# Two gate chunks at a time: a third weight sum made by an adding transfer, and kept quads taken back behind the remainders

## The chip, the cores and the metric

The kernel runs on one core of a Trainium2 chip. The metric is device microseconds from start to end of one execution. The core has four compute engines that run side by side, each with its own queue of instructions that are issued in order: TensorE (PE, matmuls), VectorE (DVE), ScalarE (ACT) and GpSimd (POOL). SyncE (SP) issues most of the transfers. A transfer that adds to what lies in its destination is issued by GpSimd here, a plain load by SyncE; both are carried by the core's 16 DMA engines.

## The reference, cut to what matters

One layer of an encoder for 256 tokens of width 2048: an input projection of the normed input h feeds a retention and a gated delta rule; both are gated, merged and projected; then cross-attention and an MLP. The change touches the gates. Each gate is a matmul of h with 2048 columns of the weights, behind which a silu or a sigmoid scales one branch:

```python
proj = h @ w_in
...
yr = jax.nn.silu(rg.astype(f32)) * yr.reshape(b, s, RET_HEADS * RET_DV)
...
yg = jax.nn.silu(gz.astype(f32)) * yg.reshape(b, s, GDN_HEADS * GDN_DV)

merged = jax.nn.sigmoid(gate_a.astype(f32)) * yr + jax.nn.sigmoid(gate_b.astype(f32)) * yg
return merged.astype(h.dtype) @ w_out
```

All data are f32.

## The kernel before

**Numbers in two parts.** To keep f32 precision, each operand of a matmul is split: ScalarE rounds it to a high part (whi, "the rounding"), VectorE subtracts that to get the low part (wlo, "the remainder"), and TensorE runs three matmuls (high by high, high by low, low by high). A half of a raw weight tile, 128 x 1024, so costs ScalarE one instruction and VectorE one, and there are three buffers for high and three for low halves.

**Tiling.** Tokens are two tiles of 128. The weights of the gates (w_chunks) come in chunks of 512 columns, each in four quarters ("quads") of 512 rows, 1 MB a quarter. The input h lies in SBUF as four quads h1[0] to h1[3], already split.

**Two chunks at once (two_chunks, L949).** In four places two chunks that read the same h, of a silu gate and of a sigmoid gate, are computed together. Quads 2 and 3 of both are multiplied plainly (plain, L1009: 24 matmuls of 512 columns for each). Quads 0 and 1 are multiplied by Strassen's scheme in Winograd's form: with the two token tiles, the two quads and the two chunks as 2 x 2 blocks, seven products (product, L1002: 12 matmuls each) stand in for eight. For that, sums of tokens (s_in) and sums of weights are needed. The weight sums are held in two f32 tiles of two halves each, x (xa, xb) and y (ya, yb). There are four of them, named in the argument moved: "x1" is x = chunk 1 quad 0 plus chunk 0 quad 0; "x2" adds chunk 1 quad 1 to x; "x4" adds chunk 0 quad 1 to x; "y" is y = chunk 1 quad 0 plus chunk 1 quad 1. (The signs lie in the token sums and in what is read from them.)

A sum is made in one of two ways. add_to (L973) has VectorE add the raw tile, which is loaded anyway, to x or y: two instructions on 128 x 1024. add_parts (L968) has GpSimd issue two transfers of 512 KB, one for each half, that read the weights from HBM once more and add them to the tile in SBUF. Before the change x2 and x4 are always adding transfers, x1 is one in the last of the four calls alone, and y is always added by VectorE (L1057).

The order in a call is: plain of chunk 0 quad 2; product with b11; product with x after x1; plain of chunk 0 quad 3; product with b22; product with x after x2; plain of chunk 1 quad 2; product with b21; product with y; product with x after x4; plain of chunk 1 quad 3. TensorE's instructions are chained in this order (triple, L995, issue_after).

**The four calls.** of_retention calls two_chunks for j = 1, 2, 3 (the gates of the retention), of_delta_rule for j = 3 (the last call, which follows the third one at once). The last call alone has `before`, which is take_back (L1124): the merged quads of the first three groups of heads were put away as f32 tiles (kept), and take_back(1) to take_back(3) split them again into high and low parts, one ScalarE (L1127) and one VectorE instruction (L1128) on 128 x 1024 each, in new quad buffers. The output projection (w_out, L1222, matmuls at L218) follows the last call and reads the three quads and a fourth one.

**What sets the order of instructions.** A planner orders the instructions of each engine at build time: among those that its model takes as ready, the one of highest priority goes first, and an engine then runs its queue in that order. Rounding, remainder and loads have the highest priority (`high_priority(offset=100000)`), gates a lower one (50000), and the take-backs none. `tc.issue_after(ins)` queues what is traced in it behind `ins` on the same engine. behind() (L95) does so for the newest rounding, remainder and raw load, kept in `latest`.

Of the kernel before, what the change touches and what calls it, by code (L numbers as in the profile page):

```python
# [31 lines left out]
H_RV, H_RG, H_GZ, H_TA, H_TB = 0, 4, 8, 12, 16  # L32
# [22 lines left out]
def trunk(ctx: ExitStack, tc: tile.TileContext, x_f, mem_f, positions, lead_f, small_f, w_blocks, w_chunks, w_ga,  # L55
# [38 lines left out]
    @contextmanager  # L94
    def behind():  # L95

        with ExitStack() as orders:
            for ins in latest.values():
                orders.enter_context(tc.issue_after(ins))
            yield  # L100

    def step():
        if steps and next(steps[0], steps) is steps:
            steps.pop(0)
# [92 lines left out]
    def cols(w, c):  # L197
        return lambda q: w[c, q]
# [79 lines left out]
    def to_feature(src, quad):  # L278

        for f2 in range(2):  # L280
            ps = bank()
            pv = ps.rearrange("p (f s) -> p f s", f=2)
            for f in range(2):
                for t in range(NT):
                    pe.transpose(pv[:, f, t * P:(t + 1) * P], src(t, f2 * 2 + f), ident)
            if not isinstance(quad, tuple):
                act.activation(quad[:, f2 * 2:f2 * 2 + 2, :], pv, AF.Copy)
                continue
            split([a[:, f2 * 2:f2 * 2 + 2, :] for a in quad], pv)
# [656 lines left out]
        vec.tensor_add(sv[:, 3], a12, sv[:, 1])  # L946
        split([a[:, i, :] for a in s_in], xs[:, 1, :])

    def two_chunks(chunks, evacs, before=None, moved=("x2", "x4")):  # L949

# [3 lines left out]
        x, y = ([mx.tile([P, 1024], F32, name=n, tag=tag, bufs=1) for n, tag in these]  # L956
                for these in ((("xa", "kq"), ("xb", "lw")), (("ya", "qk"), ("yb", "tw"))))
        opened, ends = set(), []

        def lines(n, q, h):  # L960
            return w_chunks[chunks[n], q][:, h * 1024:(h + 1) * 1024]
# [6 lines left out]
        def add_parts(to, n, q):  # L968
            with tc.high_priority(offset=100000):
                for h in range(2):  # L970
                    pool.dma_start(to[h], lines(n, q, h), accum_op=ALU.add)

        def add_to(to, src):  # L973
            with tc.high_priority(offset=100000):
                for h in range(2):
                    with tc.issue_after(latest["lo"]):
                        vec.tensor_add(to[h], to[h], src[h])

        def load(n, q):
            raw = wp.tile([P, 4 * 512], F32, name="raw", tag="raw", bufs=3)  # L980
            with tc.high_priority(offset=100000):
                fetched.append(nc.sync.dma_start(raw, w_chunks[chunks[n], q]).ins)
            return raw[:, 0:1024], raw[:, 1024:2048]

        def parted(srcs):
            halves = []
            with tc.high_priority(offset=100000):
                for src in srcs:
                    hi, lo = (h[:, :1024] for h in half_tiles())
                    latest["hi"] = act.activation(hi, src, AF.Copy).ins  # L990
                    latest["lo"] = vec.tensor_sub(lo, src, hi.bitcast(F32)).ins  # L991
                    halves.append([a.rearrange("p (k n) -> p k n", n=512) for a in (hi, lo)])
            return halves

        def triple(o, lhs, rhs, key):  # L995
            for l, r in ((0, 0), (0, 1), (1, 0)):
                with tc.issue_after(ends[-1]) if ends else ExitStack():
                    ins = pe.matmul(o, lhs[l], rhs[r], start=key not in opened, stop=False, skip_group_check=True).ins  # L998
                opened.add(key)
            return ins  # L1000

        def product(o, lhs, srcs, key):  # L1002
            halves = parted(srcs)
            for i in range(4):
                ins = triple(o, lhs(i), [a[:, i % 2, :] for a in halves[i // 2]], key)
            ends.append(ins)
            step()

        def plain(n, q, by_rows=False):  # L1009
            halves = parted(load(n, q))  # L1010
            for c, (i, t) in enumerate([(i, t) for t in range(NT) for i in range(4)] if by_rows else
                                       [(i, t) for i in range(4) for t in range(NT)]):
                ins = triple(own[n][t], [a[:, i, t * P:(t + 1) * P] for a in h1[q]],
                             [a[:, i % 2, :] for a in halves[i // 2]], (n, t))
                if c % 4 == 3:
                    ends.append(ins)
                    step()
# [4 lines left out]
        def summed(c):  # L1022
            return lambda i: [a[:, i, c * P:(c + 1) * P] for a in s_in]

        def kept_sum(tag, ps):
            o = mx.tile([P, 2, 512], F32, name="u", tag=tag, bufs=1)
            act.activation(o[:, 0], ps, AF.Copy)
            return o

        def finish(n, t, more):  # L1030
            with tc.high_priority(offset=50000):
                evacs[n](t, own[n][t], 0, 512, more)

        def others(q):
            if before:
                before(q)

        plain(0, 2)
        load_parts(x, 1, 0)
# [7 lines left out]
            u = kept_sum("vh", shared)  # L1047
        u1, u3 = u[:, 0], u[:, 1]
        product(p5, summed(0), x, "p5")
        add_parts(x, 1, 1)  # L1050
        plain(0, 3)
        load_parts(y, 1, 0)
        if "y" in moved:
            add_parts(y, 1, 1)
        b22 = load(1, 1)
        product(own[1][0], summed(3), b22, (1, 0))
        if "y" not in moved:  # L1057
            add_to(y, b22)
        product(shared, summed(1), x, "shared")
        add_parts(x, 0, 1)  # L1060
        with tc.high_priority(offset=50000):
            d = kept_sum("vl", shared)
        others(1)
        plain(1, 2)
        b21 = load(0, 1)
        product(own[0][0], part(1, 0), b21, (0, 0))
        finish(0, 0, u1)
        product(shared, summed(2), y, "shared")
        with tc.high_priority(offset=50000):
            act.activation(u3, shared, AF.Copy)  # L1070
            vec.tensor_sub(d[:, 0], p5, d[:, 0])
            vec.tensor_sub(d[:, 1], p5, u3)
        product(own[0][1], part(1, 1), x, (0, 1))
        finish(0, 1, u3)
        others(2)
        others(3)
        plain(1, 3, True)
        kept_back.clear()
# [3 lines left out]
    def gates():  # L1082
        def gate_of(ps, f, scale, more):
            th = mx.tile([P, 512], F32, name="gth", tag="gth", bufs=1)
            if more is not None:
                vec.tensor_add(th, ps, more)
                ps = th
            act.activation(th, ps, f, scale=scale)
            return th

        def silu_gate(y):
            def evac(t, ps, c0, c1, more=None):
                th = gate_of(ps, AF.Silu, 1.0, more)
                vec.scalar_tensor_tensor(y[:, t, :], th, 0.5, y[:, t, :], op0=ALU.mult, op1=ALU.mult)
            return evac

        def sig_gate(y, other=None):
            def evac(t, ps, c0, c1, more=None):
                th = gate_of(ps, AF.Tanh, 0.5, more)
                vec.scalar_tensor_tensor(y[:, t, :], th, 1.0, y[:, t, :], op0=ALU.add, op1=ALU.mult)  # L1100
                if other is not None:
                    vec.tensor_add(y[:, t, :], y[:, t, :], other[:, t, :])
            return evac

        def of_retention(j, yr):
            if j in (1, 2, 3):
                two_chunks((H_RG + j, H_TA + j), (silu_gate(yr), sig_gate(yr)))
                return
            chunk(h1, cols(w_chunks, H_RG + j), silu_gate(yr))
            chunk(h1, cols(w_chunks, H_TA + j), sig_gate(yr))  # L1110

        def of_delta_rule(j, yr, yg, quad, before=None):
            if j in (3,):
                two_chunks((H_GZ + j, H_TB + j), (silu_gate(yg), sig_gate(yg, yr)), before, ("x1", "x2", "x4"))
            else:
                chunk(h1, cols(w_chunks, H_GZ + j), silu_gate(yg))
                chunk(h1, cols(w_chunks, H_TB + j), sig_gate(yg, yr), before=before, cuts=2 if before else 1)
            to_feature(lambda t, f: yg[:, t, f * P:(f + 1) * P], quad)

        return of_retention, of_delta_rule  # L1120
# [11 lines left out]
    for j in range(5):  # L1132
# [14 lines left out]
        if j < 4:  # L1147
            yr = mx.tile([P, NT, 512], F32, name="yr", tag="yr", bufs=1)
            yg = mx.tile([P, NT, 512], F32, name="yg", tag="yg", bufs=1)
# [159 lines left out]
    b11, b12, b22, b21 = (a[:, c:c + 8, :].rearrange("p k s -> p (k s)") for a in (rt, tr) for c in (0, 8))  # L1309
# [341 lines left out]
```

## Time and profile before

| | |
|---|---|
| median of 3 runs | 2036.61 us (2036.29 to 2036.93) |
| the profiled execution | 2035.52 us, of which its span 2033.5 |
| TensorE clock granted | 0.999 |
| transfers by SyncE | 406.93 MB, 57.5% of 16 engines' span |
| adding transfers by GpSimd | 18 of 512 KB, 9.44 MB, 2.6% |
| HBM read | 403.38 MB |

The span is cut into instructions with start and length in microseconds. A row of a timeline has the start, the length, the engine, the line of the kernel, the operation, the tiles (written <- read), and in brackets how long the engine stood idle before it and what ended that. TensorE's matmuls overlap, so their lengths exceed the distance of their starts; a delay is read from the starts. In a table of windows each engine has its busy time, and the last two columns are the share of the DMA engines that was busy and what they moved.

### The profile page before, as it was taken

Reading aid. Unit: us, or ns where it says so; the run is one execution under the profiler, and the core shown is the slowest. Engines: PE = TensorE matmul, PEld = TensorE weight load, DVE = VectorE, ACT = ScalarE, POOL = GpSimd, SP = SyncE. Lnnn points to the kernel's source line nnn. Section 1 sums busy time; section 2 is a strip of 40 time slices with the busy share of each in tenths; the row PEclk is TensorE's granted clock in tenths of the full one; section 3 lists DMA queues with packets and bytes.
Section 4 is the critical chain, followed back from the end, with each engine's and each line's share of the span. In section 5 each row is a group of like instructions: output and inputs, shape, how many; then the busy total and the mean of one; then the engine's idle time right before and its main releaser. Section 6 shows DMA issues by size and latency. Waiting matters only on the chain.

```text
span 2033.5 us, 28629 instructions
## 1 busy us (share of the span) xinstructions
PE 2019.9 (99%) x10742; PEld 1739.4 (86%) x10742; DVE 1622.9 (80%) x2513; ACT 1240.5 (61%) x2029; POOL 58.0 (3%) x68
## 2 busy tenths in 40 slices
PE   9999999999999999999999999999999999999998
PEld 7888888988888888888878899888888888888886
DVE  5887788879877887788887766777887887888788
ACT  6655765675567555755655565566557656656665
POOL 0000000000100000000100000000000000000000
PEclk9999999999999999999999999999999999999999
DMA  8678556455845575556876654568546546554661
GB/s 332 214 269 290 178 185 204 156 186 190 256 170 182 193 242 187 187 181 233 233 237 230 211 187 164 172 217 276 207 140 238 214 154 224 193 204 173 238 232 62
DMA packets 83819, 418.89 MB, mean 206 GB/s; under 512 B 16976, under 2 KB 25056, under 8 KB 39392
## 3 DMA queue, kind: packets, MB, share of 16 engines
q1 hardware_dynamic: 80656, 406.93, 57.5%
q0 software_dynamic: 2592, 9.44, 2.6%
q8 instruction: 84, 1.38, 0.3%
q10 hardware_dynamic: 432, 0.69, 0.1%
q14 instruction: 55, 0.45, 0.1%
HBM read 403.38 MB, written 11.55 MB: 204 GB/s over the span
## 4 chain that ended last, share of the span: by engine, by line
PE 92%; DVE 5%; DMA 2%; issue 1%; ACT 1%; POOLq 0%; DVEq 0%; POOL 0%; ACTq 0%
PE s L218 52%; PE s L1397 7%; PE b L1397 7%; PE s L175 5%; PE s L176 5%; PE s L174 5%; PE s L998 3%; DVE wlo L991 1%; DMA xb<-w_chunks 1%; PE b L998 1%; PE s L407 1%; PE s L408 1%; PE s L409 1%; PE b L705 1%; PE b L835 0%
## 5 line engine op out<-in xcount | busy, mean ns | idle before, releaser
L218 PE MATMUL s<-q,whi 128*128 128x512 f32 x2824 | 971.1, 391 | 0.0
L129 ACT ACTIVATE whi<-raw 128x1024 fp32r<-128x1024 f32 x535 | 567.8, 1062 | 421.7 <-PE s L218 224.4
L130 DVE TENSOR_TENSOR wlo<-raw,whi 128x1024 fp32r<-128x1024 f32 x535 | 652.3, 1222 | 215.8 <-ACT whi L129 209.2
L218 PE MATMUL s<-q,wlo 128*128 128x256 f32 x2824 | 764.9, 281 | 0.0
L218 PEld LDWEIGHTS s<-q,whi 128*128 128x128 f32 x2824 | 521.4, 188 | 100.6
L218 PEld LDWEIGHTS s<-q,wlo 128*128 128x128 f32 x2824 | 528.6, 188 | 13.3 <-DVE wlo L130 0.2
L175 PE MATMUL s<-wlo,q 128*128 128x512 f32 x448 | 176.4, 394 | 0.0
L176 PE MATMUL s<-whi,q 128*128 128x512 f32 x448 | 174.6, 390 | 0.0
L174 PE MATMUL s<-whi,q 128*128 128x512 f32 x448 | 159.0, 390 | 0.0
L227 ACT ACTIVATE bo<-s 128x256 f32<-128x256 f32 x192 | 73.2, 381 | 108.8 <-PE s L218 108.8
L1397 PE MATMUL s<-whi,q 128*128 128x512 f32 x384 | 122.1, 389 | 0.0
L228 DVE TENSOR_TENSOR bo<-bo,s 128x256 f32<-128x256 f32 x192 | 79.9, 416 | 40.3 <-ACT bo L227 39.8
L998 PE MATMUL s<-whi,q 128*128 128x512 f32 x320 | 101.4, 390 | 0.0
L174 PEld LDWEIGHTS s<-whi,q 128*128 128x128 f32 x448 | 84.0, 188 | 17.6
L175 PEld LDWEIGHTS s<-wlo,q 128*128 128x128 f32 x448 | 84.2, 188 | 16.9 <-DVE wlo L130 0.3
L176 PEld LDWEIGHTS s<-whi,q 128*128 128x128 f32 x448 | 84.2, 188 | 16.7
L1420 DVE TENSOR_TENSOR wlo<-rt,whi 128x1024 fp32r<-128x1024 f32 x55 | 67.4, 1226 | 35.9 <-ACT whi L1419 35.4
L218 PE MATMUL s<-q,whx 128*128 128x512 f32 x248 | 86.6, 390 | 0.0
L1397 PEld LDWEIGHTS s<-whi,q 128*128 128x128 f32 x384 | 72.1, 188 | 15.0
L1419 ACT ACTIVATE whi<-rt 128x1024 fp32r<-128x1024 f32 x55 | 58.4, 1061 | 41.6 <-PE s L1397 29.3
L991 DVE TENSOR_TENSOR wlo<-raw,whi 128x1024 fp32r<-128x1024 f32 x56 | 67.9, 1222 | 11.8 <-ACT whi L990 11.6
L990 ACT ACTIVATE whi<-raw 128x1024 fp32r<-128x1024 f32 x56 | 59.0, 1059 | 28.6 <-PE s L998 15.7
(403 smaller groups left out, 2975.4 us busy)
## 6 DMA issues: line engine op xcount, KB each, us to landing
raw<-w_ff SPq DMA_DIRECT2D x96, 1024.0 KB
raw<-w_chunks SPq DMA_DIRECT2D x76, 1024.0 KB
raw<-w_blocks SPq DMA_DIRECT2D x64, 1024.0 KB
raw<-w_xk SPq DMA_DIRECT2D x16, 1024.0 KB
raw<-w_out SPq DMA_DIRECT2D x16, 1024.0 KB
raw<-w_xq SPq DMA_DIRECT2D x16, 1024.0 KB
raw<-w_xo SPq DMA_DIRECT2D x16, 1024.0 KB
rt<-w_ff SPq DMA_DIRECT2D x16, 1024.0 KB
```

The costliest lines, as they stand in the source:

```text
L129: latest["hi"] = act.activation(hi[:, cs], src[:, cs], AF.Copy).ins
L130: latest["lo"] = vec.tensor_sub(lo[:, cs], src[:, cs], hi[:, cs].bitcast(F32)).ins
L174: pe.matmul(o, xh, wh, start=first, stop=False)
L175: pe.matmul(o, xh, wl, start=False, stop=False)
L176: pe.matmul(o, xl, wh, start=False, stop=last)
L218: ins = pe.matmul(ps[b][:, :S] if part else ps[b], halves[h][part][:, i, b * P:(b + 1) * P], x[:, kk % 4, :], start=kk == 0 and not part, ...
L227: act.activation(o, ps[b][:, S:], AF.Copy)
L228: vec.tensor_add(o, o, ps[b][:, :S])
L991: latest["lo"] = vec.tensor_sub(lo, src, hi.bitcast(F32)).ins
L998: ins = pe.matmul(o, lhs[l], rhs[r], start=key not in opened, stop=False, skip_group_check=True).ins
L1397: ins = pe.matmul(o, lhs[l], rhs[r], start=key not in opened, stop=last and j == 2, skip_group_check=True).ins
L1420: latest["lo"] = vec.tensor_sub(lo, raw[:, c:c + 1024], hi.bitcast(F32)).ins
```

## The change

The third sum, y, becomes an adding transfer in all four calls: y is in the default of moved, and in the set of the last call, which so has all four. The call of take_back(1) moves from ahead of the plain product of chunk 1 quad 2 to behind the product with y, and all three take-backs are traced inside behind(). The branches on "x2" are new too; every call's set holds "x2".

```diff
-    def two_chunks(chunks, evacs, before=None, moved=("x2", "x4")):
+    def two_chunks(chunks, evacs, before=None, moved=("x2", "x4", "y")):
...
             if before:
-                before(q)
+                with behind():
+                    before(q)
...
         product(p5, summed(0), x, "p5")
-        add_parts(x, 1, 1)
+        if "x2" in moved:
+            add_parts(x, 1, 1)
         plain(0, 3)
         load_parts(y, 1, 0)
         if "y" in moved:
             add_parts(y, 1, 1)
         b22 = load(1, 1)
         product(own[1][0], summed(3), b22, (1, 0))
+        if "x2" not in moved:
+            add_to(x, b22)
         if "y" not in moved:
             add_to(y, b22)
...
-        others(1)
         plain(1, 2)
         b21 = load(0, 1)
         product(own[0][0], part(1, 0), b21, (0, 0))
         finish(0, 0, u1)
         product(shared, summed(2), y, "shared")
+        others(1)
...
-                two_chunks((H_GZ + j, H_TB + j), (silu_gate(yg), sig_gate(yg, yr)), before, ("x1", "x2", "x4"))
+                two_chunks((H_GZ + j, H_TB + j), (silu_gate(yg), sig_gate(yg, yr)), before, ("x1", "x2", "x4", "y"))
```

others(q) calls before(q) where there is one.

## The prediction

> **What bounds the kernel now.** I read the page first: busy shares and chain, to see who sets the time.
>
> ```profile
> PE 2019.9 (99%) x10742; PEld 1739.4 (86%) x10742; DVE 1622.9 (80%) x2513; ACT 1240.5 (61%) x2029; POOL 58.0 (3%) x68
> PE 92%; DVE 5%; DMA 2%; issue 1%; ACT 1%; POOLq 0%; DVEq 0%; POOL 0%; ACTq 0%
> ```
>
> TensorE is busy for 99% of the span and is 92% of the chain. Work taken off VectorE is worth only the TensorE waits that it ends, so I looked for those waits in the four calls of two_chunks (from 523.9, 739.3, 954.1 and about 1001 us). Next, the timeline of TensorE there: the matmuls with idle time before them, for three the matmul ahead.
>
> ```profile
> 548.49 0.50 PE L998 MATMUL b<-wlo,sh 128*128 128x512 f32 x1 [0.17 <-DVE wlo L991]
> 763.67 0.50 PE L998 MATMUL b<-wlo,sh 128*128 128x512 f32 x1 [0.16 <-DVE wlo L991]
> ...
> 977.85 0.40 PE L998 MATMUL s<-whi,sl 128*128 128x512 f32 x1
> 978.09 0.39 PE L998 MATMUL b<-whi,sh 128*128 128x512 f32 x1
> 978.64 0.50 PE L998 MATMUL b<-wlo,sh 128*128 128x512 f32 x1 [0.16 <-DVE wlo L991]
> 978.98 0.40 PE L998 MATMUL b<-whi,sl 128*128 128x512 f32 x1
> ...
> 1027.72 0.39 PE L998 MATMUL b<-whi,sh 128*128 128x512 f32 x1
> 1028.69 0.50 PE L998 MATMUL b<-wlo,sh 128*128 128x512 f32 x1 [0.58 <-DVE wlo L991]
> ...
> 1039.53 0.40 PE L998 MATMUL b<-whi,sh 128*128 128x512 f32 x1
> 1040.84 0.50 PE L998 MATMUL b<-wlo,sh 128*128 128x512 f32 x1 [0.92 <-DVE wlo L991]
> ```
>
> Undisturbed, starts lie 0.24 us apart (977.85 to 978.09). From 978.09 to 978.64 are 0.55, from 978.64 to 978.98 0.34: this wait costs 0.31 + 0.10 = 0.4 us, and 548.49 and 763.67 are its like in the first two calls. In the last call, 1027.72 to 1028.69 costs 0.73, and 1039.53 to 1040.84 costs 1.07; with the same 0.10 behind each, 0.8 and 1.2. All five together are 3 x 0.4 + 0.8 + 1.2 = 3.2 us: what this change can win at most here, under 0.2% of the time (4.1 us), which is about what a measurement of this kernel can tell from no change.
>
> Then what makes them wait: VectorE's and ScalarE's timelines of the third and the last call.
>
> ```profile
> 975.09 1.22 DVE L977 TENSOR_TENSOR ya<-ya,raw 128x1024 f32<-128x1024 f32 x1
> 976.22 1.22 DVE L977 TENSOR_TENSOR yb<-yb,raw 128x1024 f32<-128x1024 f32 x1
> 977.36 1.22 DVE L991 TENSOR_TENSOR wlo<-xa,whi 128x1024 fp32r<-128x1024 f32 x1
> ...
> 1027.41 1.22 DVE L991 TENSOR_TENSOR wlo<-xb,whi 128x1024 fp32r<-128x1024 f32 x1 [1.01 <-ACT whi L990]
> ...
> 1037.84 1.22 DVE L1128 TENSOR_TENSOR q<-mg,q 128x1024 fp32r<-128x1024 f32 x1
> 1038.97 0.69 DVE L1086 TENSOR_TENSOR gth<-s,u 128x512 f32<-128x512 f32 x1
> 1039.57 1.22 DVE L991 TENSOR_TENSOR wlo<-yb,whi 128x1024 fp32r<-128x1024 f32 x1
> ```
>
> ```profile
> 974.59 1.06 ACT L990 ACTIVATE whi<-xa 128x1024 fp32r<-128x1024 f32 x1 [1.66 <-PE s L998]
> 976.89 1.06 ACT L990 ACTIVATE whi<-xb 128x1024 fp32r<-128x1024 f32 x1 [0.86 <-PE s L998]
> ...
> 1026.32 1.06 ACT L990 ACTIVATE whi<-xb 128x1024 fp32r<-128x1024 f32 x1 [1.85 <-DMA xb<-w_chunks]
> ...
> 1040.26 1.06 ACT L990 ACTIVATE whi<-xb 128x1024 fp32r<-128x1024 f32 x1 [0.75 <-DMA xb<-w_chunks]
> ```
>
> Three different causes. At 978.64 the y adds (L977) stand ahead of the remainder of xa. At 1040.84 a take-back (L1128) and a gate stand ahead of the remainder of yb. At 1028.69 no VectorE work is to blame: ScalarE stood idle 1.85 us until the adding transfer of xb had landed.
>
> **The change part by part.** First the third sum in the three calls of the retention. Two adds of 1.22 us leave VectorE in each. The rounding of xa ends at 974.59 + 1.06 = 975.65, so its remainder can end at 976.9, before TensorE's 978.3; next is that of xb, possible from 977.95 to 979.2, used at 979.7. All three waits go: 3 x 0.4 = -1.2 us. What comes instead are adding transfers, whose price the trace shows by those of x: their issues in GpSimd's timeline, then the summary of their line (L971), then the table of windows.
>
> ```profile
> 965.41 0.90 POOL L971 DMA_DIRECT2D xa<-w_chunks  x1 [1.04 <-DVE mv L922]
> ...
> 1015.05 0.89 POOL L971 DMA_DIRECT2D xa<-w_chunks  x1 [9.97 <-DVE wlo L991]
> 1016.73 0.87 POOL L971 DMA_DIRECT2D xb<-w_chunks  x1 [0.79 <-DVE wlo L991]
> 1026.70 0.85 POOL L971 DMA_DIRECT2D xa<-w_chunks  x1 [9.10 <-DVE wlo L991]
> 1028.93 0.86 POOL L971 DMA_DIRECT2D xb<-w_chunks  x1 [1.39 <-DVE wlo L991]
> ```
>
> ```profile
> DMA to landing us min/median/max: 5.5/7.7/11.2
> ```
>
> ```profile
> core 0: us, PE busy (x) PEld busy (x) DVE busy (x) ACT busy (x) POOL busy (x), PEclk, DMA share, GB/s
> 968.50:972.50 4.00, 4.00 (x19) 3.33 (x18) 3.85 (x10) 3.13 (x7) 1.15 (x1) 1.00 1.07 212
> 1015.00:1018.00 3.00, 3.00 (x15) 2.42 (x14) 2.73 (x3) 2.86 (x5) 1.75 (x2) 1.00 1.00 423
> 950.00:960.00 10.00, 10.00 (x53) 8.55 (x52) 7.97 (x11) 6.55 (x10) 0.00 (x0) 1.00 0.85 314
> 960.00:970.00 10.00, 10.00 (x55) 8.59 (x55) 9.82 (x25) 7.20 (x14) 3.99 (x4) 1.00 0.60 156
> 1005.00:1040.00 35.00, 34.28 (x148) 27.23 (x146) 28.72 (x31) 22.36 (x24) 3.54 (x5) 1.00 1.01 311
> 1040.00:1045.00 5.00, 4.16 (x18) 3.43 (x19) 5.00 (x6) 4.08 (x5) 0.00 (x0) 1.00 0.16 64
> 1045.00:1050.00 5.00, 5.00 (x24) 4.03 (x23) 4.56 (x6) 2.22 (x3) 0.00 (x0) 1.00 0.48 152
> ```
>
> With adding transfers alone in flight (968.5 to 972.5) full queues move 212 GB/s, with plain loads (1015 to 1018) 423: an added byte holds the queues twice as long. A pair for one sum is 2 x 512 KB = 1.05 MB, so 4.9 us of all queues. Between 950 and 970 they are free for 10 x 0.15 + 10 x 0.40 = 5.5 us: the pair fits. GpSimd, 3% busy, pays 0.9 us for each issue; behind a y transfer that waits for its load queue the x transfers, for which ScalarE's rounding waits, and the rsqrt of the group norm, for which VectorE waits. I take -1.2 us. If the cover fails, xa (965.41) lands after the longest 11.2 us, at 976.6, not by 974.59: +2 us a call, +6 in the three.
>
> The last call is another case: from 1005 to 1040 the queues are full (1.01), and the pair adds 4.9 us to them. The Trainium skill (DMA: Bandwidth & Descriptors, "Issuing engines are not separate DMA queues") says that transfers issued by GpSimd share the same 16 engines with all others, which speaks against moving the sum here; the full share above agrees. Whose landing slips depends on the order on GpSimd's queue. Two rows bear on it, the y loads in SyncE's timeline and the summary of the take-backs' line.
>
> ```profile
> 1001.99 0.56 SPq L966 DMA_DIRECT2D ya<-w_chunks  x1
> 1002.60 1.24 SPq L966 DMA_DIRECT2D yb<-w_chunks  x1
> ```
>
> ```profile
> L1127 ACT ACTIVATE q<-mg x3: 1048/1052/1061, 488.8 to 1036.6; 128x1024 fp32r<-128x1024 f32 x3
> ```
>
> The last row shows how the planner orders: a take-back that the source writes in the last call stands at 488.8, because its input was ready. So the y pair, which waits only for the y load, is placed when that load is due. From 1001.6 the queues owed a raw load and y, 2.10 MB at 423 GB/s = 5.0 us, and the pair of x1, 4.9 us: y landed near 1011.5, an estimate from these rows. The second x pair is issued at 1015.05 and 1016.73, when xa and xb have been read. The y pair would thus go first, by 3 to 4 us. With the queues to itself it takes 4.9 us and delays the x pair by 4.9 - 3.5 = 1.4; sharing them half and half with plain loads, 9.8 - 3.5 = 6.3, and 7 if the x pair is slowed too. I take the middle, 4.0 us, since plain loads hold about half of that window (311 GB/s lies halfway between 212 and 423). Rounding of xb already waits for this landing (1026.32), so it reaches TensorE one for one: +4.0 us (1.4 to 7).
>
> The take-backs. Behind the remainder of yb, L1128 no longer stands ahead of it: that remainder follows the one of ya at once, 1.7 us sooner, and the wait at 1040.84 goes: -1.2 us. Next late there is the fourth transfer (1040.26, 0.75 waited); as all that comes before it has slipped by 4 us, its issue has too, but it then meets emptier queues (0.16 from 1040), so I charge nothing; its price uncovered is 0.7. What is moved: three times 1.05 us on ScalarE and 1.22 on VectorE, of which 488.8 and the second (about 1017) were hidden. All now queue behind the remainders near 1040, where VectorE is busy 5.00 and 4.56 of 5 us, and their quads are the first three that the output projection reads from 1050 on. Two of the three, 2.4 us, are new to this stretch. In 1040 to 1050 VectorE has 0.44 us free. Between nothing (the projection needs the second and third quad later than the first) and 2.4 - 0.4 = 2.0, I take +0.5, near the lower end as only the first is needed at once. The branches on "x2" change nothing: all calls hold it. POOL's and SP's other queues are not passed.
>
> Sum: -1.2 + 4.0 - 1.2 + 0.5 = **+2.1 us**. The profiled execution took 2035.5 us, 1.1 under the median of 2036.6; the same step on the median gives **2038.7 us**, no difference by the 0.2% bound.
>
> **Rivals.**
>
> A, the y pair hides. If it lands inside its head start or lies where nothing waits, the last call costs nothing and the waits go: -1.2 - 1.2 + 0 to 0.5, so 2034.2 us. For it: y is not read until about 1035, and 3.5 us of head start cover most of 4.9. Against: the full queues. The Trainium skill (the same page, "Anatomy of one DMA — SWDGE (gpsimd) path") gives such a transfer 2.0 us plus its bytes at 436 GB/s, an estimate of 3.2 us for 512 KB; by it the pair would be over within its head start and this rival would come true. The rows differ: the shortest landing is 5.5 us.
>
> B, slower: the y pair shares the queues to its end in the last call. The rounding of xb, then all of TensorE's order behind it, waits. It decides from an x delay of 6.1 us on, as -1.2 + 6.1 - 1.2 + 0.5 = 4.2; at 7 us with the 2.0 of the tail it is +6.6, 2043.2 us. For it: 1.01 over 35 us, and three landings of xb already waited for.
>
> C, the x pair goes first. Then x stays as it is (the wait of 0.8 remains) and the fourth pair, issued at 1026.70, stands behind y. The queue is 4.9 us longer at 1028.93 and its landing slips by that; TensorE would have come 1.2 us sooner there, so +4.9 - 1.2 of it shows against before, less the 1.2 of the retention: +2.5, 2039.1 us, or less, as the output projection's loads can yield. Against: x2 waits for its readers, y does not.
>
> D, the edit doesn't do what it says: the planner, given other ready times, lays out other stretches anew, and that outweighs the rest. The nearest row is the take-back at 488.8, placed far from its source line; no wait stands at it, so the lower price is nothing, and the upper one that of all five waits quoted, some 3 us or a little more, either way.
>
> **How the numbers follow.** Forecast (x delayed by 1.4 to 6 us, total -0.5 to +4.1) 0.42; A 0.20; B 0.25; C 0.10; D 0.03. The range runs from A's 2034.2, lowered to 2033.9 for D, to B's 2043.2: it leaves out most of D, a B beyond its price and a failing cover in the retention. Faster by over 0.2% needs more than all five waits: only D, 0.03. Slower is B, 0.25. The rest, 0.72, is no difference.
>
> **What would show it.** No L977 on y; eight more adding transfers on GpSimd, y ahead of the second x in all calls. The waits near 548, 763, 978 and 1040 gone. The rounding of xb near 1026 waiting for its DMA by 4 us more, and TensorE behind it. L1127 all after 1035. Wrong if that rounding waits no longer than now (then A), if it waits over 6 us more (then B), or if TensorE's starts in the first three calls still show the gap, or a new one at xa.

## The result, and the profile after

| | before | after |
|---|---|---|
| median of 4 runs | 2036.45 us (2036.29 to 2036.93) | 2046.92 us (2046.34 to 2047.68) |
| ratio, 95% interval | | 1.0051 (1.0034 to 1.0069) |
| the profiled execution | 2035.52 us, span 2033.5 | 2046.34 us, span 2044.3 |
| TensorE clock granted | 0.999 | 0.997 |

The kernel became slower by 10.5 us, where I had forecast +2.1 and a range up to 2043.2. The take-backs are L1131 (ScalarE) and L1132 (VectorE) from here on.

First the page of the kernel after: engines, the queue of the adding transfers, and the two lines of the chain.

```profile
PE 2023.4 (99%) x10742; PEld 1742.8 (85%) x10742; DVE 1616.1 (79%) x2505; ACT 1238.3 (61%) x2029; POOL 65.0 (3%) x76
...
q0 software_dynamic: 3744, 13.63, 3.7%
...
PE 95%; DVE 2%; DMA 2%; issue 1%; ACT 0%; POOL 0%; POOLq 0%; DVEq 0%; SPq 0%; ACTq 0%
PE s L218 52%; PE s L1401 7%; PE b L1401 7%; PE s L175 5%; PE s L176 5%; PE s L174 5%; PE s L998 4%; PE b L998 2%; DMA xa<-w_chunks 1%; PE s L407 1%; PE s L408 1%; PE s L409 1%; PE b L802 1%; DMA ya<-w_chunks 1%; PE b L705 1%
```

The edit did what it says: VectorE has 8 instructions fewer, GpSimd 8 more, and its transfers moved 13.63 MB instead of 9.44. That is all the busy shares tell. The chain by line tells more: it runs through adding transfers of ya and then of xa.

TensorE's timeline shows the price. Three places of the kernel after: the third call, the product with x2 in the last call, and the end of the last call.

```profile
977.96 0.39 PE L998 MATMUL b<-whi,sh 128*128 128x512 f32 x1
978.20 0.40 PE L998 MATMUL b<-wlo,sh 128*128 128x512 f32 x1
...
1025.23 0.39 PE L998 MATMUL s<-whi,sl 128*128 128x512 f32 x1
1032.79 0.79 PE L998 MATMUL b<-whi,sh 128*128 128x512 f32 x1 [7.18 <-ACT whi L990]
1034.05 0.79 PE L998 MATMUL b<-wlo,sh 128*128 128x512 f32 x1 [0.47 <-DVE wlo L991]
1034.65 0.63 PE L998 MATMUL b<-whi,sl 128*128 128x512 f32 x1
1035.07 0.63 PE L998 MATMUL b<-whi,sh 128*128 128x512 f32 x1
...
1037.68 0.39 PE L998 MATMUL b<-whi,sh 128*128 128x512 f32 x1
1037.91 0.40 PE L998 MATMUL b<-wlo,sh 128*128 128x512 f32 x1
...
1050.62 0.50 PE L998 MATMUL s<-wlo,q 128*128 128x512 f32 x1 [0.90 <-DVE wlo L991]
...
1055.07 0.50 PE L218 MATMUL s<-q,whi 128*128 128x512 f32 x1 [1.41 <-ACT whi L129]
1055.76 0.50 PE L998 MATMUL s<-wlo,q 128*128 128x512 f32 x1 [0.19 <-DVE wlo L991]
```

At 978.20 the remainder is there in time: the start lies 0.24 us behind the one before, the wait of the retention is gone. At 1032.79 there is a new one of 7.18 us, and the matmuls behind it (1034.65, 1035.07) come 0.42 us apart, half the pace of those from 1037.68 on. At 1050.62 and 1055.07 stand two more waits that the kernel before does not have.

What the 7.18 us waited for, in the timelines of GpSimd and of ScalarE:

```profile
1013.71 0.89 POOL L971 DMA_DIRECT2D ya<-w_chunks  x1 [9.21 <-DMA ya<-w_chunks]
1015.03 0.86 POOL L971 DMA_DIRECT2D yb<-w_chunks  x1 [0.43 <-issue]
1015.56 1.20 POOL L971 DMA_DIRECT2D xa<-w_chunks  x1
1016.25 1.40 POOL L971 DMA_DIRECT2D xb<-w_chunks  x1
```

```profile
1031.69 1.06 ACT L990 ACTIVATE whi<-xa 128x1024 fp32r<-128x1024 f32 x1 [10.49 <-DMA xa<-w_chunks]
1034.44 1.06 ACT L990 ACTIVATE whi<-xb 128x1024 fp32r<-128x1024 f32 x1 [1.70 <-DMA xb<-w_chunks]
...
1049.19 1.99 ACT L1131 ACTIVATE q<-mg 128x1024 fp32r<-128x1024 f32 x2
...
1053.97 1.04 ACT L129 ACTIVATE whi<-raw 128x1024 fp32r<-128x1024 f32 x1
```

The y pair stands ahead of the x pair, by 1.9 us only (1013.71 to 1015.56). Before, xb was issued at 1016.73 and rounded at 1026.32, 9.6 us later; now it is 1016.25 and 1034.44, 18.2 us. The summary of the transfers has, as its last number, the time from issue to landing:

```profile
ya<-w_chunks POOLq DMA_DIRECT2D x1, 512.0 KB, 8.1
yb<-w_chunks POOLq DMA_DIRECT2D x1, 512.0 KB, 11.5
xa<-w_chunks POOLq DMA_DIRECT2D x1, 512.0 KB, 16.0
xb<-w_chunks POOLq DMA_DIRECT2D x1, 512.0 KB, 18.1
```

So the y pair landed at 1021.8 and 1026.5, the x pair at 1031.6 and 1034.4. Before the change the x pair landed at 1022.5 and 1026.2 (7.4 and 9.5 us behind its issues). The y pair now has the x pair's place, and the x pair comes a whole pair later.

The end of the call is told by VectorE's timeline, and the whole by a table of windows:

```profile
1048.22 1.22 DVE L1132 TENSOR_TENSOR q<-mg,q 128x1024 fp32r<-128x1024 f32 x1
1049.35 1.22 DVE L991 TENSOR_TENSOR wlo<-xa,whi 128x1024 fp32r<-128x1024 f32 x1
...
1051.62 2.35 DVE L1132 TENSOR_TENSOR q<-mg,q 128x1024 fp32r<-128x1024 f32 x2
```

```profile
core 0: us, PE busy (x) PEld busy (x) DVE busy (x) ACT busy (x) POOL busy (x), PEclk, DMA share, GB/s
1005.00:1040.00 35.00, 27.36 (x111) 21.28 (x110) 18.93 (x21) 16.51 (x18) 5.21 (x6) 0.90 0.95 273
1032.00:1036.00 4.00, 2.74 (x6) 1.85 (x7) 1.69 (x2) 2.30 (x3) 0.85 (x1) 0.50 0.38 58
1050.00:1060.00 10.00, 7.72 (x30) 5.46 (x31) 9.90 (x12) 5.65 (x8) 0.00 (x0) 1.00 0.16 38
```

A take-back (1048.22) now stands ahead of the remainder of xa, for which TensorE waits at 1050.62; two more stand ahead of what the next projection needs, and VectorE is busy 9.90 of 10 us. And in 1032 to 1036 the granted clock is 0.50: the half pace seen above.

### The profile page after: what moved, and what is told of

The parts are those of the page before. It is cut to its first block, busy times and chain, and to the rows that moved or that the text cites. A ratio compares the mean times of both kernels' runs of the same rounds, so it can differ in the third digit from the quotient of the medians.

```text
span 2044.3 us, 28646 instructions
## 1 busy us (share of the span) xinstructions
PE 2023.4 (99%) x10742; PEld 1742.8 (85%) x10742; DVE 1616.1 (79%) x2505; ACT 1238.3 (61%) x2029; POOL 65.0 (3%) x76
## 3 DMA queue, kind: packets, MB, share of 16 engines
q0 software_dynamic: 3744, 13.63, 3.7%
## 4 chain that ended last, share of the span: by engine, by line
PE 95%; DVE 2%; DMA 2%; issue 1%; ACT 0%; POOL 0%; POOLq 0%; DVEq 0%; SPq 0%; ACTq 0%
PE s L218 52%; PE s L1401 7%; PE b L1401 7%; PE s L175 5%; PE s L176 5%; PE s L174 5%; PE s L998 4%; PE b L998 2%; DMA xa<-w_chunks 1%; PE s L407 1%; PE s L408 1%; PE s L409 1%; PE b L802 1%; DMA ya<-w_chunks 1%; PE b L705 1%
## 5 line engine op out<-in xcount | busy, mean ns | idle before, releaser
L129 ACT ACTIVATE whi<-raw 128x1024 fp32r<-128x1024 f32 x535 | 566.9, 1060 | 420.2 <-PE s L218 218.9
L175 PE MATMUL s<-wlo,q 128*128 128x512 f32 x448 | 176.1, 393 | 0.0
L1401 PE MATMUL s<-wlo,q 128*128 128x512 f32 x192 | 74.7, 389 | 0.0
```

Source lines behind the costliest of these rows:

```text
L129: latest["hi"] = act.activation(hi[:, cs], src[:, cs], AF.Copy).ins
L175: pe.matmul(o, xh, wl, start=False, stop=False)
```

## The experiments

**The theories.** ORDER: the y pair, ahead of the x pair on GpSimd's queue, makes x late. BYTES: the last call has 1.05 MB more of adding transfers than its queues carry, whatever their order. TAKE-BACKS: the take-backs, which now crowd the end, cost most of it. For each kernel the table has the stretches by TensorE's starts: how much longer each took than in the kernel before (us, one profiled execution each). "x2" goes from the product with b22 to the end of that with x after x2, "tail" from the last plain product on; P12 is the plain product of chunk 1 quad 2. "Elsewhere" is the part ahead of the last call, without the three retention waits; it moves without the change too, by +0.69 in e4 and +1.43 in e11, whose code up to there is that of the kernel before. A ratio is to the kernel before, run on the same chip; each has its 95% interval.

| kernel | retention | elsewhere | up to b22 | x2 | P12, b21 | y | x4 | tail | sum |
|---|---|---|---|---|---|---|---|---|---|
| after | -1.29 | +0.71 | +0.04 | +8.96 | 0 | -1.20 | +1.18 | +2.46 | +10.9 |
| e1, last call without y | -1.29 | +0.22 | 0 | +0.95 | 0 | -1.20 | +1.18 | +3.75 | +3.6 |
| e2, y behind x | -1.29 | +0.78 | +0.05 | +0.83 | 0 | -1.20 | +4.34 | +3.74 | +7.2 |
| e3, take-backs as before | -1.29 | +0.62 | 0 | +9.91 | +0.55 | -0.01 | -0.03 | +0.05 | +9.8 |
| e4, take-backs alone | 0 | +0.69 | 0 | +2.70 | +1.11 | -1.20 | +1.18 | +3.75 | +8.2 |
| e5, retention alone | -1.29 | +1.78 | +0.23 | -0.01 | 0 | 0 | 0 | 0 | +0.7 |
| e6, third take-back behind | -1.29 | +1.92 | 0 | -0.03 | +0.03 | -1.20 | +0.24 | +1.90 | +1.6 |
| e7, y pair plain | -1.29 | -0.60 | 0 | +8.45 | +1.44 | -1.20 | +1.18 | +3.77 | +11.7 |
| e8, y for x1 | -1.29 | +2.46 | +1.00 | +3.89 | +1.33 | 0 | 0 | 0 | +7.4 |
| e10, third on GpSimd | -1.29 | +0.16 | +0.01 | +0.13 | +0.03 | +0.48 | +0.11 | 0 | -0.4 |

**e1: the last call without the y pair.** From the kernel after:

```diff
-... before, ("x1", "x2", "x4", "y"))
+... before, ("x1", "x2", "x4"))
```

> The changed kernel, but in the last call y is added by VectorE again; the retention calls keep their adding transfer of y, the take-backs stay behind. Theory ORDER (in the last call the y pair stands ahead of the second x pair on GpSimd's queue, so x lands 8 to 9 us late) and theory BYTES (4.9 us more for queues that are full, wherever they stand) both expect the 9 us lost at the second x product to go: 2046.9 - 9.0 = 2037.9 us, up to 2038.6 if the old 0.7 us wait there returns; the adding transfer of x landing about 9.5 us after its issue instead of 18. Theory TAKE-BACKS (the moved take-backs cost the time, the x wait is their consequence) expects it to stay over 2044.

Measured: 2041.48 us, ratio 1.0016 (1.0007 to 1.0026). Of the +8.96 at x2 +0.95 is left, so the y pair caused it. But the kernel is still slower than before, and some 3 us over what ORDER and BYTES expected. In the trace it is the end of the call that is left:

```profile
1042.07 0.50 PE L998 MATMUL s<-wlo,q 128*128 128x512 f32 x1 [0.90 <-DVE wlo L991]
1046.52 0.50 PE L218 MATMUL s<-q,whi 128*128 128x512 f32 x1 [1.41 <-ACT whi L129]
1047.22 0.50 PE L998 MATMUL s<-wlo,q 128*128 128x512 f32 x1 [0.19 <-DVE wlo L991]
```

These are the same three waits as in the kernel after, without any y pair: they belong to the take-backs. The tail is longer by 1.3 us than there, and e1's table of windows says why: the clock (the number ahead of the DMA share) fell to 0.50 behind them.

```profile
1044.54:1047.95 3.41, 1.81 (x7) 0.99 (x6) 3.41 (x5) 1.93 (x3) 0.00 (x0) 1.00 0.00 0
1047.95:1051.36 3.41, 3.41 (x9) 2.62 (x9) 3.28 (x4) 0.63 (x1) 0.00 (x0) 0.50 0.41 103
```

**e2: the y pair behind the x pair**, in the last call, by order on GpSimd's queue. From the kernel after:

```diff
-            add_parts(y, 1, 1)
+            add_parts(y, 1, 1, latest["adds"] if before else None)
```

Here latest["adds"] is the last transfer of x2, and add_parts issues its own behind it.

> The changed kernel, but in the last call the y pair is queued on GpSimd behind the second x pair; all transfers and their bytes stay. ORDER expects x to land as early as before the change and 8 to 9 us of the loss to go: about 2038 us. BYTES expects the 4.9 us to come back at the next product that needs an adding transfer, the fourth sum of x behind y: 2041 to 2043 us, with ScalarE's rounding of xb there waiting 3 to 5 us for its DMA.

Measured: 2042.61 us, ratio 1.0021 (1.0011 to 1.0030). GpSimd's timeline shows the new order, ScalarE's the rounding of xb for x2 and for x4:

```profile
1014.54 0.88 POOL L971 DMA_DIRECT2D xa<-w_chunks  x1 [9.98 <-DVE wlo L991]
1016.18 0.86 POOL L971 DMA_DIRECT2D xb<-w_chunks  x1 [0.76 <-DVE wlo L991]
1016.72 1.19 POOL L971 DMA_DIRECT2D ya<-w_chunks  x1
1017.26 1.55 POOL L971 DMA_DIRECT2D yb<-w_chunks  x1
```

```profile
1026.69 1.06 ACT L990 ACTIVATE whi<-xb 128x1024 fp32r<-128x1024 f32 x1 [2.69 <-DMA xb<-w_chunks]
...
1043.90 1.06 ACT L990 ACTIVATE whi<-xb 128x1024 fp32r<-128x1024 f32 x1 [3.62 <-DMA xb<-w_chunks]
```

With the same bytes, xb is rounded 10.5 us behind its issue instead of 18.2, and x2 costs +0.83 as without a y pair: ORDER makes the x2 delay. The four transfers (7.3, 10.4, 14.9 and 17.1 us from issue to landing) landed at 1021.8, 1026.6, 1031.6 and 1034.4, the same times as in the kernel after, with the pairs exchanged: GpSimd's transfers land one behind another, in the order of their issue. The bytes do not vanish, though: x4 comes late instead, +4.34 against e1's +1.18. That is 3.2 us, moved to the next product, as rival C had it. They are not bytes alone: the pair of x4 now stands right behind the y pair (its first packet at 1033.07, y's last at 1033.05), so this run does not tell bytes and order apart there.

**e3: the take-backs as before**, the rest of the change kept. From the kernel after:

```diff
-                with behind():
-                    before(q)
+                before(q)
...
+        others(1)
         plain(1, 2)
...
-        others(1)
```

> The changed kernel with the take-backs where they were before the change; y is an adding transfer in all four calls. ORDER and BYTES expect the 9 us at the second x product to stay and the 2.5 us lost from the last plain product into the output projection to go, while the wait at the remainder of yb (1.2) comes back: 2046.9 - 2.5 + 0 to 1.2 = 2044.4 to 2045.6 us. TAKE-BACKS expects 2036 to 2038.

Measured: 2045.95 us, ratio 1.0037 (1.0023 to 1.0050). Tail and x4 are as before, x2 stays at +9.9: TAKE-BACKS as the main cause falls.

**e4: the moved take-backs alone**, the reverse of e3's edit put into the kernel before.

> The kernel before with the moved take-backs alone; no sum is moved. ORDER and BYTES expect the second x product as before and the loss of the stretch behind it alone: 2036.5 - 1.2 (wait at yb gone) + 1.2 (wait at xa behind it) + 2.5 (start of the output projection) = 2039 us. If the 2.5 us came from the lateness of x and not from the take-backs: 2035 to 2036.5. TAKE-BACKS expects over 2044.

Measured: 2041.82 us, ratio 1.0019 (1.0010 to 1.0028). The three parts at the end are e1's to 0.01 us: -1.20, +1.18, +3.75. The +2.70 and +1.11 at x2 and behind it belong to a late x pair in this execution, the slowest of ten, with no y pair and an unchanged queue; without it the parts sum to +3.7 us, near the 3.9 of the ratio. The expectation had 2.5 for the tail; it is 3.75, with half pace as in e1.

**e5: the retention's part alone.** e1's and e3's edits together.

> The changed kernel with only the part in the retention left: its three calls take the third sum by adding transfers, the last call keeps three adding pairs, and the take-backs stand where they stood before. If the retention's -1.3 us (three waits of 0.43 us) is a real gain and everything that cost time came from the last call and the take-backs, this runs 1.3 us under the kernel before in its trace's marks, and the median is 2035 to 2036 us against 2036.5. If the adding transfers in the retention cost something that the marks do not show (clock, queues of the next groups), it is at or above the kernel before.

Measured: 2036.47 us, ratio 0.9998 (0.9990 to 1.0007). The waits are gone in the marks (-1.29). The +1.78 elsewhere is little more than the +1.43 that e11 has there without the change; whether a part of it is a price of the adding transfers stays open. The times of the whole cannot tell a gain of 1.3 us from nothing.

**e6: the third take-back alone behind the remainders**, on e5.

```diff
-                before(q)
+                with behind() if q == 3 else ExitStack():
+                    before(q)
```

> The last kernel plus one edit: the third of the three take-backs of the last call alone is put behind the remainders, the first two stay where they stood. TAKE-BACKS as a matter of how many are queued up near the output projection: with one instead of three there the wait at yb's remainder stays gone (-1.2 us against the last kernel), and of the +1.2 at the remainder of xa and the +3.75 at the output projection little is left, 0 to 1.2 in all; total -1.2 to 0 against the kernel with the retention's part alone. If instead a single take-back in that place is enough to hold the remainder of xa and the first rounding of the output projection, the -1.2 is given back and more: total +1.2 to +3.8 against it.

Measured: 2036.89 us, ratio 0.9997 (0.9989 to 1.0006). One take-back wins 1.20 at y and gives back 0.24 + 1.90 behind it: even one is too many there. It lies between the two expectations.

**e8: the y pair instead of the first x pair.** e5 with the set of the last call changed, so three adding pairs as before:

```diff
-... before, ("x1", "x2", "x4"))
+... before, ("x2", "x4", "y"))
```

> The kernel with the retention's part alone, but in the last call the y pair is an adding transfer and the first x pair is not (VectorE does that add from a plain load): three adding pairs as before, so the same bytes added, with the y pair still free to go ahead of the second x pair on GpSimd's queue. BYTES alone: the queues owe 4.9 us less than in the changed kernel, so the second x pair lands as before and x2 starts within 1 us of its place. ORDER: the y pair still stands ahead; if y's load lands at about 1013 us as it does in the changed kernel, x2 comes 3 to 9 us late again. If y lands sooner, since the first pair does not hold the queues, the y pair is through in time and ORDER too says under 2 us. GpSimd's issue times tell which of these it was.

Measured: 2040.78 us, ratio 1.0017 (1.0008 to 1.0025). GpSimd's timeline:

```profile
1009.67 0.90 POOL L971 DMA_DIRECT2D ya<-w_chunks  x1 [5.10 <-ACT whi L990]
...
1017.50 0.84 POOL L971 DMA_DIRECT2D xa<-w_chunks  x1 [5.67 <-DVE wlo L991]
```

The y pair now has 7.8 us of head start and as many bytes are added as before, yet x2 costs +3.89 and its slow matmuls 1.33 more. Both theories had said less (under 1, under 2): even so long a lead doesn't take a pair of y out of the way. Its packets ran from 1013.7, 4.0 us behind the issue, to 1021.5, and those of the x pair began right behind, at 1021.6. The product with x1 costs another 1.00 with its sum made by VectorE.

**e7: the y pair as a plain transfer** in the last call, the same bytes to the same tiles, in the same place of the queue. From the kernel after, with the sum of y left out there:

```diff
-                    pool.dma_start(to[h], lines(n, q, h), accum_op=ALU.add)
+                    pool.dma_start(to[h], lines(n, q, h), accum_op=op)
...
-            add_parts(y, 1, 1)
+            add_parts(y, 1, 1, ALU.bypass if before else ALU.add)
```

> The changed kernel, whole, but in the last call the y pair on GpSimd's queue is a plain transfer of the same bytes from memory to the same tiles, in the same place of the queue, without adding: y's sum is left out there, so its output is not the reference's. It measures what the adding costs the x pair behind it. If the pair's cost is the queue time of its bytes, 2.5 us of all queues at 423 GB/s instead of 4.9 at 212, the second x pair lands about half as late: x2 +3 to +5 us instead of +9. If the cost is that GpSimd's transfers are served one behind the other, each at its own pace whatever it does, x2 stays 7 to 9 us late. If adding is all of it, x2 is late by under 2 us.

Measured: 2047.43 us, ratio 1.0049 (1.0036 to 1.0062). ScalarE's timeline, behind an issue at 1015.99:

```profile
1031.84 1.06 ACT L990 ACTIVATE whi<-xb 128x1024 fp32r<-128x1024 f32 x1 [3.32 <-DMA xb<-w_chunks]
```

From issue to rounding, xb takes 15.9 us: 2.3 less than in the kernel after, close to the 2.5 us of queue time by which the prediction's rates set plain and adding apart, but still 6.3 more than before. Nearly three quarters of the delay are there without any adding. The packets show that the nearness to 2.5 is chance: the plain pair is through in 3.9 us (1015.9 to 1019.8) where the adding one takes 6.8 in the kernel after, but the x pair behind it takes 11.2 instead of 9.4 us, while 2.10 MB of plain loads pass beside it instead of 1.57. x2 gains little by it (+8.45), as the shorter waits are followed by more matmuls at half pace.

**e10: the remainder of the third take-back on GpSimd**, on e5; the attempt at a version that beats both.

```diff
-            vec.tensor_sub(back[1], kept[q - 1], back[0].bitcast(F32))
+            (pool if q == 3 else vec).tensor_sub(back[1], kept[q - 1], back[0].bitcast(F32))
```

> The kernel with the retention's part alone (three adding pairs in the last call, take-backs where they stood), and the remainder of the third take-back is made by GpSimd instead of VectorE. If what cost time at the remainder of yb is that VectorE has no free 1.2 us there, this wait (0.92, with the matmul behind it 1.2 us) goes and nothing takes its place: 1.2 us under the kernel with the retention's part alone in the marks, 2.5 under the kernel before, ratio about 0.9988 and the first version that is faster than both. If GpSimd is slow at it (its row of one operation on a tile as large is not in the trace of before) and the output projection's third quad comes late, or the two engines hold each other up, the gain is given back at the output projection, 0 to +3 us.

Measured: 2036.88 us, ratio 0.9996 (0.9987 to 1.0005). The wait at yb did not go, it grew from 0.92 to 1.41 us. TensorE's, GpSimd's and VectorE's timelines:

```profile
1040.38 0.50 PE L998 MATMUL b<-wlo,sh 128*128 128x512 f32 x1 [1.41 <-DVE wlo L991]
```

```profile
1036.74 2.50 POOL L1131 TENSOR_TENSOR q<-mg,q 128x1024 fp32r<-128x1024 f32 x1 [7.80 <-ACT q L1130]
```

```profile
1037.98 2.35 DVE L991 TENSOR_TENSOR wlo<-yb,whi 128x1024 fp32r<-128x1024 f32 x1
```

VectorE's subtraction, begun while GpSimd's was under way, took 2.35 us instead of 1.22 and ended 1.09 us behind it. No version here is faster than the kernel before by more than the measurement can tell.

**e11: waits put where there were none.** On the kernel before, ScalarE repeats the rounding of the first half of seven loads of w_xo:

```diff
-            halves = fetch(w[c, g], k, n, at=AT_BLOCKS)
+            halves = fetch(w[c, g], k, n, at=AT_BLOCKS, more={1: 1, 3: 2, 5: 3, 7: 4, 9: 5, 11: 6, 13: 8}.get(c * (KT // k) + g, 0) if w is w_xo else 0)
```

> The kernel before, with waits of TensorE of several lengths put where it has none: in the projection behind the cross attention (the 16 loads of w_xo) the rounding of the first half of seven loads is repeated 1, 2, 3, 4, 5, 6 and 8 times more by ScalarE, 1.06 us each, with the same result. It measures the clock by itself: what the matmuls behind a wait cost. If the half pace seen behind the late transfers (0.43 us from start to start instead of 0.23) belongs to the length of the wait alone, matmuls behind waits under about 1.5 us run at full pace and those behind longer ones at half pace for a few us, costing some 1.6 us more whatever the length. If it belongs to the transfers or to the place and not to the wait, no matmul behind any of the seven is slowed, and a wait costs its own length.

Measured: 2070.53 us. One and two repeats were hidden; the five others gave waits of 2.1, 3.3, 4.2, 5.0 and 7.1 us. TensorE's timeline at the shortest (128x512 and 128x256 are matmuls of 512 and of 256 columns):

```profile
1284.11 0.73 PE L218 MATMUL s<-q,whi 128*128 128x512 f32 x2 [1.89 <-ACT whi L129]
1285.06 1.22 PE L218 MATMUL s<-q,whi 128*128 128x512 f32 x2 [0.22 <-ACT whi L129]
...
1286.51 0.63 PE L218 MATMUL s<-q,whi 128*128 128x512 f32 x1
...
1287.15 0.63 PE L218 MATMUL s<-q,whi 128*128 128x512 f32 x1
```

From 1286.51 to 1287.15 are 0.64 us for a pair, one of 512 and one of 256 columns, that takes 0.35 at the same line in the kernel before (1051.05 to 1051.40). Behind all five waits the starts are stretched so, in stretches of 3.4 or 6.8 us of granted clock 0.50, and the time lost beside the waits is 1.6, 1.6, 1.6, 2.7 and 2.2 us. No transfer is late there: the half pace belongs to the wait. The shortest waits are hidden here, so their part of the expectation was not tried.

## Why the prediction was wrong, point by point

- **Retention, -1.2:** right in the marks: -1.29 in every kernel that holds it; the cover did not fail in any. The time of e5 as a whole cannot show it.
- **"The y pair would thus go first, by 3 to 4 us":** the order was right, the lead was not. It was 1.9 us, since y landed at 1013.7 and not "near 1011.5": I had added up what the queues owed at the rates of full queues, and they took 2.2 us longer. My own sum for half shares, 9.8 less the lead, gives 7.9 with the true lead at issue.
- **"I take the middle, 4.0 us":** the step that failed. xb came 8.6 us later behind its issue (18.2 against 9.6), past the upper end of 7. The middle comes to 7.5 us for the y pair, less a head start of 3.5. The head start was worth nothing. The y pair was issued at 1013.7, while the x pair would have been issued near 1014.5 (1015.05 before, in an execution that reaches the last call 0.6 us later): a lead of 0.8 us, not 3.5. The y pair's first packet then came 3.8 us behind its issue, where the x pair's had come 3.0 behind: the 0.8 are gone. From that packet on, 1017.46 to 1024.26, a row of GpSimd's queue has (packets, MB, share of the 16 engines):

```profile
q0 software_dynamic: 280, 1.05, 77.5%
```

  These 1.05 MB are the y pair, in 6.8 us; the packets of the x pair begin right behind, at 1024.27. The x pair itself takes 9.4 us from its first packet to its last instead of 7.3, while 1.57 MB of plain loads pass beside it instead of 0.98. 6.8 + 2.2 = 9.0, near the +8.96 at x2. This is rival B's mechanism, beyond its price, since B too took the head start off.
- **The clock, not in the prediction:** behind the wait the matmuls run at half pace until 1037.47, but this costs little at x2. The eighth of the product's twelve starts at 1036.81, as VectorE is done with the remainder of xb at 1036.76 (before: 1028.69 behind 1028.63), and half pace ahead of it passes in waiting. From the eighth to the end of the product are 1.57 us instead of 1.27: 0.3 us of the +8.96. What half pace costs where nothing else is waited for, e11 shows.
- **The wait at yb, -1.2:** right as a term (-1.20), but taken back at once. "Next late there is the fourth transfer ... I charge nothing": next late was not the transfer but the remainder of xa, behind a take-back that behind() let in there: +1.18, e1 and e4 alike.
- **Tail, +0.5 (0 to 2.0):** mis-sized. e1, e2 and e4 measure +3.75, the kernel after +2.46. I had bounded it by VectorE's free time and left out that ScalarE's take-backs stand ahead of the first rounding of the output projection (1049.19 and 1053.97 above), and in e1, e2 and e4 the half pace.
- **The sum:** -1.3 + 9.0 - 1.2 + 1.2 + 2.5 = +10.2, and +0.7 elsewhere, against +2.1.

The same waits (1.41 and 0.19) are followed by half pace in e1 and by full pace in the kernel after. The clock's records settle why. In each trace the clock changes only at times that lie a whole number of stretches of 3.413 us apart. In e1 one such stretch, 1044.54 to 1047.95 (shown above), holds both waits, and TensorE is busy for 1.81 of 3.41 us: the clock falls. In the kernel after an edge at 1054.54 cuts the longer wait in two:

```profile
1051.12:1054.54 3.42, 2.54 (x11) 1.72 (x10) 3.42 (x5) 3.42 (x6) 0.00 (x0) 1.00 0.02 5
1054.54:1057.95 3.41, 2.63 (x9) 1.64 (x10) 3.41 (x5) 0.48 (x1) 0.00 (x0) 1.00 0.00 0
```

Neither stretch is as idle as that, and the clock stays at 1.00. Where the edges lie against the work differs from trace to trace, so the 1.3 us by which the tail of the kernel after is shorter than e1's are luck.

## What to carry to other kernels

A transfer moved to a queue that holds another transfer on the critical path is priced by the whole time of what then stands ahead, at the rate of the stage with full queues, and not by a share of it. A head start counts from where the other transfer would have begun without the first. Ask first which of the two is due sooner. Work put off past a late instruction is late for the next one: follow it until a stretch where the engine has room. A wait of TensorE of 2 us or more cost, in all five of e11, its length and 1.6 us or more on top.

## What the runs showed of the hardware

- **The clock changes on a grid of 3.41 us, behind stretches that are half idle.** In e11 the granted clock falls to 0.50 at 1284.76, 1301.83, 1318.90, 1335.96 and 1356.44, all a whole number of 3.413 us apart, and holds for one or two such stretches. In all twelve traces, between 30 and 2020 us, every stretch of this grid at full clock in which TensorE was idle for 1.77 us or more was followed by 0.50, none with 1.50 or less was, and of five with 1.60 to 1.64 three were. So single waits of 1.41 us (e10 at 1040.38) and 1.21 (e6) were followed by full pace. The Trainium skill (TensorE: Matmul & The Clock Gate, "Part 1: The HAM clock gate") states half rate after at least one idle window of about 3.4 us, and full rate again after a busy one of as long. The length of the window agrees (3.41 us from 1284.76 to 1288.18 in e11); the fall came from less idle time here (1.89 of 3.41 us). That its window runs freely, as the page says, agrees with the different places of the edges in e1 and in the kernel after.
- **GpSimd's transfers land one behind another.** Four transfers of 512 KB, issued within 2.7 us, landed at 1021.8, 1026.5, 1031.6 and 1034.4 (after) and at 1021.8, 1026.6, 1031.6 and 1034.4 (e2), in both in the order of their issue.
- **A subtraction on GpSimd held VectorE's up.** For 128x1024 f32 it took 2.50 us on GpSimd, and VectorE's, begun beside it, 2.35 us instead of 1.22 (e10). No run shows GpSimd's alone.
